# Moving the fourth GDN head behind all input projection tiles, and the late modulation vectors into the attention, in a two-layer hybrid transformer trunk

## The chip, the core and the metric

The kernel runs on one core of a Trainium2 chip. The metric is device time in microseconds (us) of one execution. The kernel before took 3876.38 us, the median of three runs that lay between 3871.95 and 3881.77 us.

In the text PE is TensorE (the matrix engine), PEld its weight loads, DVE is VectorE, ACT is ScalarE, POOL is GpSimd, and SP is the engine that issues nearly all DMAs (transfers to and from memory), in one queue and in order.

## The reference, cut to what matters

Each of two layers mixes tokens in three parallel ways from one input projection, and an MLP follows. There are 1024 latent tokens and 256 context tokens, 1024 features, all in fp32.

```python
for l in range(DEPTH):                      # DEPTH = 2
    sh1, sc1, gt1, sh2, sc2, gt2 = adaln(c, w_ada[l], b_ada[l])      # six modulation vectors
    h_lat = rms_norm(x, g_attn_pre[l]) * (1.0 + sc1) + sh1
    # hybrid_mixer: p = h @ w_in, split by columns into
    #   GDN  : 4 heads of 128, gated delta rule in chunks, forward and backward
    #   LRU  : a linear recurrence over 256 channels, forward and backward
    #   MLA  : 4 heads of attention over 1280 keys
    y_lat = concat([gdn_out, rl * gelu(..), a_l]) @ w_out
    x = x + gt1 * rms_norm(y_lat, g_attn_post[l])
    h = rms_norm(x, g_mlp_pre[l]) * (1.0 + sc2) + sh2
    x = x + gt2 * rms_norm(sq_relu_mlp(h, w_mlp1[l], w_mlp2[l]), g_mlp_post[l])
```

The first two of the six vectors (shift and scale, numbers 0 and 1) are needed before the input projection. Numbers 2 (gate), 3 and 4 (shift and scale of the MLP's norm) are first needed after the output projection of the same layer; number 5 later still. The context takes the same path, with vectors of its own, and its output is not needed in the second layer.

## The kernel before, in words

Activations lie transposed, features on the 128 partitions, tokens along the row, in three blocks: "c" (256 context tokens), 0 and 1 (512 latent tokens each). A large matmul is three fp32r products of high and low parts (`mm3`, line 230): eight contraction steps times three products, 24 matmuls for each block, 72 for a tile of 128 output features over all three blocks. A weight tile is loaded by SP (`wr`, two buffers), split by ACT into `wh` and by POOL into `wl` (line 138).

The order of instructions on each engine is fixed when the program is built. A scheduler places them by priority, and priority follows the order in which the Python code emits the operations. A stretch under `later()` gives its priority back, so the operations emitted in it are interleaved with those that follow.

Start. The three blocks are normalized, then `ada_pe` (line 260 on) computes modulation vectors 0 and 1: for each of eight contraction steps and each vector one `wa` load of 512 KB and two matmuls of 32x512 (line 273), at the end four transposes (line 283). A list `self.bg` holds such steps in waiting; `tick(n)` (line 322 on) adds n to a counter `self.due` and runs as many steps as it allows. At the start `tick(99)` runs the 17 steps of vectors 0 and 1. Then `run` puts the 26 steps of vectors 2, 3 and 4 into `bg`, to be run by later ticks: `weight` ticks with `self.rate` (0 in this stage), `mla_attend` ticks 1 for each of its key chunks (line 1022).

Mixer (lines 1033 to 1142). There are 24 input projection tiles: one with the GDN's gates, four per GDN head (`tiles(h)`: k, q, v and the output gate z), two pairs for the LRU (`xtile`), and three for the attention's latents (`kvq`: one for keys and values, two for queries). In layer 1 two gelu tiles and one z tile stand ahead of the rest. Tiles k, q, v go through a convolution on DVE (line 147), SiLU and transposes (line 441 and 460), and to memory.

`head(h)` is the gated delta rule of one head: decay matrices (lines 622 to 646), inversion of ten triangular 128x128 matrices per direction (`gdn_invert`; its core is a forward substitution of 60 dependent DVE operations on `X` and `T`, lines 138), ten steps of scan per direction (`gdn_scan`, lines 764 to 788, each a chain PE, DVE, PE, ACT, PE), and `gdn_y` with the transposes of line 819. It uses PSUM banks a, b and c.

`lru` has 20 segments of 256 tokens, each a chain of some 20 operations on ACT, DVE and POOL with a `lr<-lx` load in front and, in the first ten, an `lh<-lr` store behind (line 881). `mla_open` and `mla_prep(h)` prepare keys, queries, values and the row maxima of head h (26 DVE reductions per head in layer 0, 24 in layer 1, line 983), `mla_attend(h)` computes scores (lines 1012 to 1014), exponentials on ACT and the product with V (line 1027), 22 chunks per head in layer 0 and 20 in layer 1. After the GDN heads and the attention the output projection reads all eight groups of features.

Before the change the mixer emits: `tiles(0) head(0) tiles(1) head(1) tiles(2) head(2) xtile(0) xtile(1) tiles(3) head(3) kvq()`, then `mla_open`, `mla_prep(0)`, the LRU (under `later`), `mla_prep(1)`, `mla_attend(0)` and so on. So each head's chain runs beside the projection tiles emitted after it.

Of the kernel before, what the change touches and what calls it, by code (L numbers as in the profile page):

```python
# [43 lines left out]
class Trunk:  # L44
# [277 lines left out]
    def tick(self, n):  # L322

        self.due = self.due + n if self.bg else 0
        with self.later():
            while self.bg and self.due >= 1:
                self.due -= 1
                self.bg.pop(0)()


    def S(self, n):
# [701 lines left out]
    def mixer(self, L, hs, obl):  # L1033

        nc = self.nc
        l, last = L.l, L.l == DEPTH - 1
        pk = {}
        other = "left" if self.side == "right" else "right"
        sp = self.sp = self.pool("sp", other)
        yd = [self.dram(f"y{i}") for i in range(8)]  # L1040

        d = pk["krba"] = self.dram("krba")
        ba = sp.tile([P, NCH, 16], F32, name=self.nm("ba"))

        def evac(b, ps):
            c0, w = GRP[b]
            t = self.T()[:, :ps.shape[-1]]
            self.act(t, ps)
            self.keep(d, b, t)
            pt = self.G((P, 4, P))  # L1050
            for i in range(w):
                nc.tensor.transpose(pt[:, i, 0:32], t[0:32, i * P:(i + 1) * P], self.ident[0:32, 0:32])
            nc.vector.tensor_copy(ba[:, c0:c0 + w, :], pt[:, 0:w, 0:16])
        self.cur = ("s", (self.tp, 4), ["st"])
        zd = [self.dram(f"z{h}") for h in range(NH)]
        lg = [self.dram(f"lg{t}") for t in range(2)]

        if l:
            for t in range(2):
                self.gelu_tile(L, hs, 6 + t, obl, lg[t])  # L1060
            self.z_tile(L, hs, 8, obl, zd[0])
        self.w_in_tile(L, hs, 0, [0, 1, "c"] if l else BL, evac)
        self.gdn_coeffs(L, ba)
        gp = self.gp = self.pool("gp", other)
        self.XAT = gp.tile([P, NCH, 64], F32, name=self.nm("XAT"))
        nc.gpsimd.memset(self.XAT, 0.0)
        kd, xg = [], []

        def tiles(h):
            i0 = 12 + 3 * h  # L1070
            kd.append((self.qk_tile(L, hs, i0, 3 * h + 1, BL, f"k{h}", True),
                       self.qk_tile(L, hs, i0 + 1, 3 * h, obl, f"q{h}"),
                       self.v_tile(L, hs, i0 + 2, 3 * h + 2, BL, f"v{h}")))
            if h or not l:
                self.z_tile(L, hs, 8 + h, obl, zd[h])

        def head(h):
            with self.actor("g", (gp, 2), ["c"]):
                o = self.gdn_head(L, h, *kd[h], last)
                self.gdn_y(o, kd[h][1][1], zd[h], obl, yd[h])  # L1080

        def xtile(t):
            xg.append((self.lx_tile(L, hs, 4 + t, t, f"lx{t}"), lg[t]))
            if not l:
                self.gelu_tile(L, hs, 6 + t, obl, lg[t])

        def kvq():
            pk["kvn"] = self.kv_tile(L, hs, 1, "kvn")
            pk["cqn"] = self.cq_tiles(L, hs, 2, obl, "cqn")
        for h in range(3):  # L1090
            tiles(h)
            head(h)
        xtile(0)
        xtile(1)
        tiles(3)
        head(3)
        kvq()
        self.close(self.ap)
        side = self.side
        mp = self.mp = self.pool("mp", side)  # L1100
        self.lw = mp.tile([P, 2, 2, 2, P], F32, name=self.nm("lw"))
        nc.sync.dma_start(self.lw, self.I["lru_w"][l])
        mq = self.pool("mq", side)
        self.cur = ("s", (self.tp, 4), ["st", "b"])
        self.mla_open(L, pk, mq, not last)
        kqv = [self.mla_prep(L, 0, mq, not last)]
        self.cur, mine = self.main, self.cur
        with self.later():
            self.lru(L, [x for x, _ in xg], [g for _, g in xg], obl, yd[4:6])
        self.cur = mine  # L1110
        kqv.append(self.mla_prep(L, 1, mq, not last))
        self.mla_attend(0, kqv[0], not last, yd[6])
        kqv.append(self.mla_prep(L, 2, mq, not last))
        self.mla_attend(1, kqv[1], not last, yd[6])
        kqv.append(self.mla_prep(L, 3, mq, not last))
        self.close(mq)
        self.close(gp)
        self.close(sp)
        self.side = "left" if side == "right" else "right"
        self.ap = self.pool("ap", self.side)  # L1120
        ys = {b: [self.A(b) for _ in range(8)] for b in obl}

        def load(i):
            for b in obl:
                s, n = BLK[b]
                a = ys[b][i]
                nc.sync.dma_start(a[:, 1, :].bitcast(F32), yd[i][:, s:s + n])
                self.act(a[:, 0, :], a[:, 1, :].bitcast(F32))
                self.tt(a[:, 1, :], a[:, 1, :].bitcast(F32), a[:, 0, :].bitcast(F32), ALU.subtract, nc.gpsimd if i % 2 else None)
        for i in range(4):  # L1130
            load(i)
        self.mla_attend(2, kqv[2], not last, yd[7])
        load(4)
        load(5)
        load(6)
        self.mla_attend(3, kqv[3], not last, yd[7])
        load(7)
        self.cur = self.main
        self.close(mp)
        self.lp = self.xp = self.pool("lp", side)  # L1140
        return ys
# [290 lines left out]
```

## Time and profile before

| | us |
|---|---|
| median of three runs | 3876.38 |
| the profiled execution | 3882.76 |
| its span, first to last instruction | 3881.0 |
| PE busy | 3515.5 (91%) |
| DVE busy | 2099.4 (54%) |
| ACT busy | 1646.9 (42%) |
| POOL busy | 1315.2 (34%) |

Stages of the profiled execution, in us from the span's start, by the first and last matmul of each kind: modulation vectors on PE 26 to 123; layer 0 projection tiles 123.5 to 704; LRU, attention and the rest of head 3 until the output projection starts at 1041; MLP. Layer 1: projection tiles until 2668 (the transposes of its gate tile at 2191), LRU and attention until 3025.

How to read the profile: busy time is what an engine's instructions cover. Matmuls are pipelined, so busy PE is not PE at its peak. Releasers of a wait are inferred from semaphores. PEclk is the share of full TensorE clock that was granted. In a row of a timeline the first number is the start, the second the duration of the merged group, and in brackets stands the idle time ahead of it with what ended it. In a row of windows stand the stretch, its length, and per engine the busy time with the number of instructions, then the granted clock, the share of DMA busy and GB/s. In a row of groups stand, behind the bar, busy time, mean duration in ns, and idle time of the engine ahead of them.

### The profile page before, as it was taken

The numbers are of one execution on the slowest core, as the hardware profiler recorded it, in microseconds if no ns is written. First come the engines' busy times: TensorE is split into PE (matmuls) and PEld (weight loads), VectorE is DVE, ScalarE is ACT, GpSimd is POOL, SyncE is SP. The second block draws the span as 40 slices with busy tenths as digits, with TensorE's granted clock in tenths as the row PEclk, the third lists the DMA queues.
The fourth block names the chain that finished last, engine by engine and source line by source line (L and its number), as shares of the span: only waits on it lengthen the run. The fifth ranks groups of instructions, "written<-read, shape, count | busy, mean of one in ns | idle before, by whom it ended". The sixth has DMA issues, their size and how long they took to land. (4 is left out here: it accounts for less than half of the span.)

```text
span 3881.0 us, 51471 instructions
## 1 busy us (share of the span) xinstructions
PE 3515.5 (91%) x19236; PEld 2749.3 (71%) x19236; DVE 2099.4 (54%) x4351; ACT 1646.9 (42%) x3477; POOL 1315.2 (34%) x919
## 2 busy tenths in 40 slices
PE   4899989788998999999997989996798999999998
PEld 1577777455586888888877777774454778888886
DVE  5377677667437145555266586677676271422124
ACT  3355544555445331222354455444555463222242
POOL 3112212335476221111375421113335574222254
PEclk8899999899899999999998999997798999999999
DMA  6322212201433222322434322212002433311143
GB/s 236 120 84 82 85 59 77 81 22 49 126 114 109 66 82 87 93 90 85 130 114 130 97 85 85 80 63 97 29 18 79 145 102 96 100 47 46 49 137 102
DMA packets 164922, 347.13 MB, mean 89 GB/s; under 512 B 15552, under 2 KB 74304, under 8 KB 164672
## 3 DMA queue, kind: packets, MB, share of 16 engines
q1 hardware_dynamic: 164672, 343.85, 27.8%
q8 instruction: 151, 2.47, 0.3%
q14 instruction: 99, 0.81, 0.1%
HBM read 277.99 MB, written 65.80 MB: 89 GB/s over the span
## 5 line engine op out<-in xcount | busy, mean ns | idle before, releaser
L138 POOL TENSOR_TENSOR wl<-wr,wh 128x1024 fp32r<-128x1024 f32 x280 | 681.8, 2435 | 1703.7 <-ACT wh L135 953.1
L230 PE MATMUL mm<-A,wh 128*128 128x512 f32 (+1 forms) x3008 | 710.1, 380 | 2.9 <-POOL A L138 2.3
L135 ACT ACTIVATE wh<-wr 128x1024 fp32r<-128x1024 f32 x288 | 304.8, 1058 | 838.0 <-PE mm L230 325.8
L230 PEld LDWEIGHTS mm<-A,wh 128*128 128x128 f32 x3008 | 524.8, 195 | 97.1 <-POOL A L138 2.7
L138 DVE TENSOR_TENSOR hid<-T,hid 128x512 fp32r<-128x512 f32 (+1 forms) x160 | 171.6, 1075 | 451.6 <-ACT hid L135 451.6
L230 PE MATMUL mm<-A,wl 128*128 128x512 f32 (+1 forms) x1504 | 362.0, 374 | 1.4 <-DVE wl L138 1.4
L230 PE MATMUL mm<-hid,wh 128*128 128x512 f32 (+1 forms) x1280 | 302.7, 377 | 8.9 <-ACT T L135 6.8
L230 PEld LDWEIGHTS mm<-A,wl 128*128 128x128 f32 x1504 | 260.4, 191 | 48.4 <-DVE wl L138 1.6
L230 PEld LDWEIGHTS mm<-hid,wh 128*128 128x128 f32 x1280 | 227.7, 191 | 57.5 <-ACT T L135 7.2
L147 DVE SCALAR_TENSOR_TENSOR T<-raw,sm,T 128x512 f32<-128x512 f32 (+4 forms) x240 | 182.0, 759 | 49.3 <-ACT raw L135 25.5
L138 DVE TENSOR_TENSOR acc<-acc,mm 128x512 f32<-128x512 f32 (+1 forms) x140 | 88.5, 632 | 216.6 <-PE mm L230 215.9
L230 PE MATMUL pd<-A,wh 128*128 128x512 f32 (+1 forms) x704 | 193.7, 403 | 0.0
L230 PE MATMUL plr<-A,wh 128*128 128x512 f32 (+1 forms) x800 | 185.3, 383 | 0.0
L135 ACT ACTIVATE T<-T 128x512 f32<-128x512 f32 (+1 forms) x243 | 141.6, 583 | 98.2 <-DVE T L147 72.2
L1027 PE MATMUL pd<-Pt,V 128*128 128x512 f32 (+1 forms) x336 | 167.9, 620 | 8.8 <-ACT Pt L135 4.7
L138 POOL TENSOR_TENSOR S<-S,T 128x512 f32<-128x512 f32 (+1 forms) x126 | 162.8, 1294 | 38.0 <-ACT T L135 34.3
L230 PE MATMUL pb<-A,wh 128*128 128x512 f32 (+1 forms) x800 | 173.0, 367 | 1.2 <-ACT wh L135 1.2
L230 PE MATMUL mm<-hid,wl 128*128 128x512 f32 (+1 forms) x640 | 166.4, 378 | 8.1 <-DVE wl L138 8.1
L147 DVE SCALAR_TENSOR_TENSOR ada<-wa,sil,ada 128x256 f32<-128x256 f32 x392 | 166.3, 488 | 6.4 <-DMA wa<-in_w_ada_dram 6.4
L230 PEld LDWEIGHTS plr<-A,wh 128*128 128x128 f32 x800 | 143.6, 188 | 31.3
L230 PE MATMUL plr<-hid,wh 128*128 128x512 f32 (+1 forms) x640 | 153.2, 381 | 13.0 <-DVE hid L138 9.9
L147 DVE SCALAR_TENSOR_TENSOR lr<-lr,lr 128x256 f32<-128x256 f32 x218 | 108.3, 507 | 91.4 <-POOL lr L138 85.8
(365 smaller groups left out, 6848.1 us busy)
## 6 DMA issues: line engine op xcount, KB each, us to landing
wr<-in_w_mlp_dram SPq DMA_DIRECT2D x208, 512.0 KB, 3.6
wa<-in_w_ada_dram SPq DMA_DIRECT2D x96, 512.0 KB, 3.7
wr<-in_w_in_dram SPq DMA_DIRECT2D x48, 512.0 KB, 3.7
wr<-in_w_out_dram SPq DMA_DIRECT2D x32, 512.0 KB, 3.6
A<-y SPq DMA_DIRECT2D x32, 256.0 KB, 3.3
xm<-acc SPq DMA_DIRECT2D x32, 256.0 KB, 3.7
x<-xm SPq DMA_DIRECT2D x16, 512.0 KB, 6.4
kT<-k SPq DMA_DIRECT2D x8, 640.0 KB, 4.2
```

The source lines that it names most:

```text
L135: return self.nc.scalar.activation(out, in_, f, **kw)
L138: return (eng or self.nc.vector).tensor_tensor(out, a, b, op=op)
L147: return self.nc.vector.scalar_tensor_tensor(out, a, s, b, op0=op0, op1=op1)
L230: mm = nc.tensor.matmul(ps, w[wi][:, wk, :], a[:, ai, :], start=n == 0, stop=n == last)
L1027: nc.tensor.matmul(po, V[:, c, :], p, start=ci == 0, stop=ci == len(chunks) - 1)
```

## The change

Two edits. First, `tick` sets `due` to 0 when `bg` has run empty. Before, `tick(99)` left 82 of its 99, which the first tick of the mixer (with n = 0) spent on all 26 steps of vectors 2, 3 and 4 at once, ahead of the first projection tile. Now they wait in `bg` for the ticks of `mla_attend(0)`, and the last few for `mla_attend(1)`.

Second, the order of the mixer: `kvq` stands between `tiles(1)` and `head(1)`, `xtile(0)` ahead of `head(2)`, and `head(3)` behind everything that projects, in front of `mla_open`. The pool of the hidden states is closed, and the pools of LRU and attention opened, ahead of `head(3)`. Since head 3 uses the banks a, b and c, `mla_open` and the preparation of attention heads 0 and 1 take their PSUM tiles from banks st and d instead of st and b; from `mla_attend(0)` on it is st and b again.

```diff
             while self.bg and self.due >= 1:
                 self.due -= 1
                 self.bg.pop(0)()
+        if not self.bg:
+            self.due = 0
...
-        for h in range(3):
-            tiles(h)
-            head(h)
+
+        tiles(0)
+        head(0)
+        tiles(1)
+        kvq()
+        head(1)
+        tiles(2)
         xtile(0)
+        head(2)
         xtile(1)
         tiles(3)
-        head(3)
-        kvq()
         self.close(self.ap)
...
         mq = self.pool("mq", side)
-        self.cur = ("s", (self.tp, 4), ["st", "b"])
+        head(3)
+        self.cur = ("s", (self.tp, 4), ["st", "d"])
         self.mla_open(L, pk, mq, not last)
         kqv = [self.mla_prep(L, 0, mq, not last)]
...
         kqv.append(self.mla_prep(L, 1, mq, not last))
+        self.cur = ("s", (self.tp, 4), ["st", "b"])
         self.mla_attend(0, kqv[0], not last, yd[6])
```

On PE, at the end of vectors 0 and 1 (`pb`), the program before goes on with vectors 2 and 3 (`pc` from the loads `wa`):

```order
L273 MATMUL pb_325<-wa_386,sil 32x512 x2
L283 MATMUL pb_392<-cst,T_390 128x128 x4
L273 MATMUL pc_520<-wa_521,sil 32x512 x2
L273 MATMUL pc_520<-wa_525,sil 32x512 x2
L273 MATMUL pc_520<-wa_529,sil 32x512 x2
```

The changed program goes on with the first projection tile (`mm` from the activations `A` and the weight `wh`):

```order
L273 MATMUL pb_325<-wa_386,sil 32x512 x2
L283 MATMUL pb_392<-cst,T_390 128x128 x4
L230 MATMUL mm_526<-A_402,wh_522 128x256
L230 MATMUL mm_526<-A_406,wh_522 128x256
L230 MATMUL mm_526<-A_410,wh_522 128x256
```

48 matmuls of line 273 and 8 transposes have left this place.

On DVE, in the middle of head 3's forward substitution of layer 0 (`T<-X` and `X<-X,T` in turn), the program before mixes in the small operations of a norm (`n4s`) and a scaling (`T` with `sm`) of `kvq`:

```order
L138 TENSOR_TENSOR T_5825<-X_5776 128x234
L138 TENSOR_TENSOR n4s_6549<-n4s_6548,n4s_6550 128x4
L138 TENSOR_TENSOR X_5776<-X_5776,T_5825 128x18x13
L138 TENSOR_TENSOR n4s_6549<-n4s_6549,n4s_6548 128x4
L138 TENSOR_TENSOR T_5825<-X_5776 128x238
L147 SCALAR_TENSOR_TENSOR n4s_6548<-n4s_6549,n4s_6548 128x4
L138 TENSOR_TENSOR X_5776<-X_5776,T_5825 128x17x14
L138 TENSOR_TENSOR T_5825<-X_5776 128x240
```

The changed program mixes in the row maxima of attention head 0 (`mx`) and LRU operations (`lr`):

```order
L138 TENSOR_TENSOR T_6163<-X_6114 128x238
L147 SCALAR_TENSOR_TENSOR lr_6962<-lr_6969,lr_6962 128x256
L138 TENSOR_TENSOR X_6114<-X_6114,T_6163 128x17x14
L985 TENSOR_REDUCE mx_6854<-pd_6858 128x1
L138 TENSOR_TENSOR T_6163<-X_6114 128x240
L985 TENSOR_REDUCE mx_6854<-pst_6861 128x1
L138 TENSOR_TENSOR X_6114<-X_6114,T_6163 128x16x15
L985 TENSOR_REDUCE mx_6854<-pst_6867 128x1
```

In all, between the first and the last of the 60 operations, 26 maxima, 7 LRU operations of line 147, 2 of line 860 (862 in the changed kernel), one scan and some ten operations of rotary embedding and query splitting stand in the changed program. On PE head 3's first transposes stand directly behind the last projection matmul, and the whole preparation of attention heads 0 and 1 and the matmuls of six LRU segments stand within head 3; of the attention's own products only 20 matmuls stand ahead of its end.

On SP, during `mla_attend(0)` of layer 0, the program before has LRU loads and stores and the attention's output:

```order
L881 DMA lh_1187_7080<-lr_7229 128x256
L942 DMA wq_8476<-in_w_uq_dram 128x2x128
L842 DMA lr_7292<-lx_790_4680 128x256
L881 DMA lh_1188_7081<-lr_7264 128x256
L1031 DMA y_111_510<-T_8057 64x512
L842 DMA lr_7327<-lx_813_4892 128x256
```

The changed program has the loads `wa` of the modulation vectors between them:

```order
L883 DMA lh_1158_6961<-lr_7144 128x256
L271 DMA wa_7915<-in_w_ada_dram 128x1024
L271 DMA wa_7926<-in_w_ada_dram 128x1024
L271 DMA wa_7936<-in_w_ada_dram 128x1024
L271 DMA wa_7947<-in_w_ada_dram 128x1024
L1033 DMA y_111_510<-T_7978 64x512
L844 DMA lr_7207<-lx_856_5221 128x256
L271 DMA wa_7957<-in_w_ada_dram 128x1024
```

Such a load waits for the buffer `wr` that a matmul of an earlier step frees, and the stores and loads behind it in the queue wait with it.

## The prediction

> **What bounds the kernel now.** I read the page first, then the windows of each stage, then timelines at the stage borders, and groups of lines within the stages that the change touches. The page:
>
> ```profile
> span 3881.0 us, 51471 instructions
> PE 3515.5 (91%) x19236; PEld 2749.3 (71%) x19236; DVE 2099.4 (54%) x4351; ACT 1646.9 (42%) x3477; POOL 1315.2 (34%) x919
> PEclk8899999899899999999998999997798999999999
> ```
>
> PE is busy 91% of the span, so what can be won lies in the 365 us in which it is not. The granted clock has dips at the start and at two thirds of the span, where PE sits idle too. The windows cut by stage say where the idle time is (the numbers behind the length are busy us of PE, PEld, DVE, ACT, POOL, then clock, DMA share, GB/s). Layer 0: vectors 0 and 1; vectors 2 to 4; projection tiles; kvq with head 3, the end of these; then the first and the last part of LRU and attention, and these as a whole:
>
> ```profile
> 0.00:53.50 53.50, 23.11 (x97) 8.90 (x98) 32.05 (x115) 15.33 (x29) 13.20 (x16) 1.00 0.78 284
> 53.50:123.50 70.00, 41.86 (x107) 5.40 (x105) 24.96 (x44) 18.82 (x34) 16.76 (x14) 0.60 0.57 175
> 123.50:704.50 581.00, 532.14 (x4274) 444.02 (x4275) 388.65 (x1000) 289.26 (x837) 109.61 (x70) 0.97 0.25 82
> 620.00:704.50 84.50, 78.61 (x774) 65.75 (x773) 62.24 (x195) 34.63 (x94) 16.23 (x12) 0.98 0.19 59
> 704.50:780.00 75.50, 48.35 (x187) 30.59 (x187) 50.12 (x123) 41.47 (x111) 33.93 (x40) 0.73 0.21 69
> 860.00:1041.50 181.50, 153.12 (x485) 90.24 (x485) 122.98 (x210) 98.62 (x211) 84.84 (x107) 0.90 0.21 62
> 704.50:1041.50 337.00, 275.05 (x937) 166.68 (x937) 227.56 (x430) 184.33 (x418) 145.14 (x182) 0.87 0.18 54
> ```
>
> Layer 1: projection tiles from the gate tile on; LRU and attention; of these the stretch in which head 3 runs nearly alone; and the attention proper:
>
> ```profile
> 2191.00:2668.00 477.00, 436.09 (x3378) 356.43 (x3376) 334.62 (x859) 237.93 (x680) 79.84 (x45) 0.96 0.24 81
> 2668.00:3025.00 357.00, 275.69 (x1220) 171.93 (x1221) 241.26 (x476) 185.35 (x421) 141.68 (x171) 0.84 0.16 49
> 2668.00:2783.00 115.00, 60.44 (x515) 46.09 (x516) 81.06 (x199) 59.57 (x164) 45.43 (x57) 0.71 0.18 58
> 2806.50:3025.00 218.50, 199.78 (x676) 119.11 (x677) 144.63 (x246) 116.14 (x237) 87.63 (x103) 0.93 0.15 45
> ```
>
> Idle PE: 49 us in 581 of layer 0's projection, 41 in 477 of layer 1's; 62 in 337 and 81 in 357 of the two tails (so I call LRU and attention together). In layer 1, 55 of the 81 lie where head 3 has lost its cover. The 70 us for vectors 2 to 4 hold 42 us of PE at a clock of 0.60.
>
> **The start.** The end of the activations' last split, the pace of the vector steps, their end, the first projection matmuls, and the second tile:
>
> ```profile
> 73.07 4.77 DVE L138 TENSOR_TENSOR A<-xin,A 128x512 fp32r<-128x512 f32 x6
> 75.71 1.05 PE L273 MATMUL pc<-wa,sil 128*32 128x512 f32 x4 [1.64 <-DMA wa<-in_w_ada_dram]
> 84.37 1.92 PE L273 MATMUL pc<-wa,sil 128*32 128x512 f32 x4 [1.63 <-DMA wa<-in_w_ada_dram]
> 122.19 0.69 PE L283 MATMUL pc<-cst,T 64*128 64x64 f32 x4 [0.69 <-ACT T L135]
> 123.51 3.78 PE L230 MATMUL mm<-A,wh 128*128 128x256 f32 x16 [0.63 <-ACT wh L135]
> 140.96 0.88 PE L230 MATMUL mm<-A,wh 128*128 128x256 f32 x6
> ```
>
> ```profile
> 655.81 3.89 PE L230 MATMUL mm<-A,wh 128*128 128x512 f32 x16
> ```
>
> The activations are whole at 77.8, the projection starts at 123.5: PE waits for loads of vectors that nobody needs yet. In the changed program block c can start while blocks 0 and 1 are still split; what is left at 77.8 is at most the 8 products of block 1 with the last low parts and the 8 behind them, 16 times 0.243 us (3.89 by 16) or 4 us. So tile 1 begins near 83 in place of 141: a gain of 57. The next weight's split on POOL ends before that, as POOL's last split of `A` is over when DVE's is. If the split of the first weight gets in front of the activations' splits on POOL, it costs some us: bounds 48 to 62.
>
> **The vectors in the attention.** 24 steps and 8 transposes go where PE is the busier engine. A step is one row of x4 above: 1.05 us, or 1.92. The group says what PE paid in the old place:
>
> ```profile
> L273 PE MATMUL pc<-wa,sil 128*32 128x512 f32 x96 | 40.0, 969 | 26.1 <-DMA wa<-in_w_ada_dram 25.5 <-DVE ada L138 0.7
> ```
>
> 40 us busy, 25.5 idle for the loads. In the attention the clock was 0.90 to 0.93, so I take the fast step: 24 times 1.05 and 2 for the transposes, 27 us. Bounds: 5, if most of it fills PE's waits there, and 48, if all steps run slow. The Trainium skill, "TensorE: Matmul & The Clock Gate" (section What's actually happening), says that the clock is halved after an idle window of about 3.4 us. The two durations above, a factor of 1.8 apart, agree; by that rule alone, with a PE that goes idle around each load, the sum would have 48 in place of 27. That end is already among the bounds.
>
> The loads pass through SP's queue, and only two buffers hold them; the loads' own pace is a rival below. What waited for the vectors, the norm behind the output projection, is hundreds of us later: nothing.
>
> **Head 3 out of the projection.** Its matmuls move from the projection stage into the tail, which alone changes nothing in the sum. What changes is PE's idle time. In the projection stage 19 tiles now lie beside three heads instead of four, so each head has six or seven tiles (at 16 times 0.243 and 8 times half of it for each third of the products, about 15 us each) beside a chain of some 112 us (next part). These stages become matmul-bound. The idle time left comes from matmuls that wait for DVE's convolution, and that stays. I take 8 us less in layer 0, 4 in layer 1; bounds 25 less to 10 more in both together.
>
> **The tail.** Now head 3 starts only when the last projection matmul is issued, so its whole chain lies in the tail. Its length, from head 0, which ran beside projection tiles:
>
> ```profile
> 208.23 0.38 PE L622 MATMUL pa<-cst,gv 128*128 128x128 f32 x2
> 232.72 0.17 DVE L138 TENSOR_TENSOR T<-X 128x30 f32<-128x30 f32 x1
> 270.90 0.19 DVE L138 TENSOR_TENSOR X<-X,T 128x30 f32<-128x30 f32 x1
> 284.70 0.49 PE L768 MATMUL pa<-vt,N 128*128 128x128 f32 x2
> 320.18 0.49 PE L788 MATMUL pc<-X,at 128*128 128x128 f32 x2
> ```
>
> 24 us to the substitution, 38 in it, 14 to the scan, 36 in that: 112. In the tail DVE has other things mixed in:
>
> ```profile
> L138 DVE TENSOR_TENSOR T<-X 128x30 f32<-128x30 f32 (+14 forms) x240 | 96.8, 403 | 3.8
> L138 DVE TENSOR_TENSOR X<-X,T 128x30 f32<-128x30 f32 (+14 forms) x240 | 93.9, 391 | 3.8
> L983 DVE TENSOR_REDUCE mx<-pst 128x1 f32<-128x512 f32 (+1 forms) x52 | 30.2, 582 | 4.4 <-PE pst L982 4.0
> L147 DVE SCALAR_TENSOR_TENSOR lr<-lr,lr 128x256 f32<-128x256 f32 x110 | 54.2, 501 | 48.6 <-POOL lr L138 46.2 <-ACT lr L135 1.7
> ```
>
> The 60 operations of one head take 24 us (190.7 by 8). The order puts between them 26 maxima (15 us), ten LRU operations (5) and about ten for rotary embedding and query (estimated at 0.6 each, as the maxima, 6), so 50 us, and with waits for POOL (0.4 us per LRU operation, 48.6 by 110) 55. With LRU work in the inversion's second part (14 to 18) and maxima in the scan (36 to 43) the chain is 24 + 55 + 18 + 43 = 140 until the attention goes on. That is first late now where the projection's tiles were.
>
> What PE does in these 140 us: head 3's matmuls (about 45, an estimate: the 78.6 us busy from 620 to 704.5 less three tiles of 15 and some 7 for their norms leave 27, and half of a scan's 36 lay behind 704), two of four preparations and six of 20 LRU segments. By the groups of the tail:
>
> ```profile
> L982 PE MATMUL pst<-K,Q 96*128 96x512 f32 (+1 forms) x52 | 27.2, 524 | 13.4 <-DVE mx L983 8.6 <-DVE T L138 4.3 <-ACT Q L135 0.2
> L982 PE MATMUL pb<-K,Q 96*128 96x512 f32 (+1 forms) x52 | 27.2, 524 | 11.6 <-DVE T L138 6.5 <-DVE mx L983 3.1 <-ACT Q L135 1.8
> L956 PE MATMUL pst<-cqn,wq 128*128 128x256 f32 (+1 forms) x32 | 14.6, 588 | 10.5 <-ACT T L135 10.5
> L845 PE MATMUL plr<-lr,lw 128*128 128x256 f32 x80 | 24.8, 420 | 1.6 <-DMA lr<-lx 1.6
> ```
>
> These and smaller ones make about 95 us for all preparations: half is 47, six segments 7, so 100 us of work and 40 idle. Behind it comes the attention, whose waits were DVE's maxima (25 idle in the two rows of line 982); half of the maxima are then done. The windows give 28 us idle in 181.5 and 19 in 218.5; I take 25 and 20. So the idle time of the tail is 65 in place of 62 in layer 0 (+3). In layer 1 the chain starts alike, but less of the old one was hidden: 45 + 20 in place of 81; half of the maxima's relief was there already, so I count 10 less, not 16.
>
> **The sum.** Start -57, vectors +27, projection idle -8 and -4, tails +3 and -10: -49 us. Against the profiled execution, 3882.76, that gives 3834; it ran 6 us above the median, 3876.38, and against that it gives 3827. I take 3830. About 0.3% (12 us) is what a measurement of this kernel can tell from no change.
>
> **Rivals.** First, head 3's chain sets the tail longer than the projection gains (slower). Layer 1 of before shows a head 3 that had only LRU and preparation beside it:
>
> ```profile
> 2633.25 0.71 PE L634 MATMUL pc<-kT 128*128 128x128 f32 x4 [2.16 <-DMA kT<-k]
> 2806.81 0.63 PE L1012 MATMUL mm<-Q,K 97*128 97x512 f32 x1
> 648.12 2.43 POOL L138 TENSOR_TENSOR wl<-wr,wh 128x1024 fp32r<-128x1024 f32 x1 [7.17 <-ACT wh L135]
> 648.25 2.32 DVE L138 TENSOR_TENSOR n4s<-n4s,n4s 128x4 f32<-128x4 f32 x1
> ```
>
> 174 us from its first products to the attention's first scores. Now a second preparation is to be done in it as well. At 185 us in both layers in place of 140 and 145 the tails are 85 longer, and the kernel takes 3915. It decides from about 165 on, where the whole gain is gone. For it: the order lets only 20 products of the attention run ahead of head 3's end. Against: in layer 1 the maxima and the key products already ran late behind kvq's round trip through memory, which is now long over. Also for it: the last two rows, in which a DVE operation on four elements takes as long as POOL's operation beside it, and LRU keeps POOL busy. The Trainium skill, "SBUF — State Buffer" (Who interferes with whom), says that a DVE instruction with two inputs in SBUF and a GpSimd one that reads SBUF block each other fully; the trace agrees in this pair. Two LRU segments' worth of POOL operations, at half their 0.75 us each an estimate of 5 to 10 us per layer, would not decide it alone. Chance 0.17.
>
> Second, the vectors' loads hold up the attention. In the old place 24 steps took 69 us (53.5 to 122.9), 2.9 us a step, with the same two buffers; the order spreads them over about as much PE work, and the SP queue has LRU stores and loads between them, which wait for DVE. If PE waits one us a step and runs slow steps half of the time, this costs 35 us more: 3865, at the border of no change. Chance 0.15.
>
> Third, the new cover is better than I think: the tails' idle time falls to 45 in layer 0 and 35 in layer 1, and the projection loses 25: 3830 - 20 - 36 - 13 gives 3761. For it: the 55 us hole in layer 1. Against: DVE's chain. Chance 0.15.
>
> Fourth, the start isn't won, as the first tile waits for something else. The order has nothing in between, and the activations are there at 77.8. The kernel takes 3830 + 57, or 3887. Chance 0.03. That leaves 0.50 for the forecast, with 3805 to 3855 as its own range.
>
> **Chances and range.** Faster by over 0.3% (under 3865): the forecast, the third, and about a third of the second: 0.70. Within 0.3%: most of the rest of the second and the lower end of the first: 0.12. Slower: 0.18. The range reaches down over half of the third (3780) and up to the lower half of the first (3890).
>
> **What would show it.** Right: the first projection matmul near 60 and the second tile near 83; no `pc<-wa` before the attention; projection stages of 540 and 460 us; from the last projection matmul to the end of head 3's scan 140 us, with DVE over 80% busy in the substitution; tails of about 395 and 350 us. Wrong: a substitution of over 70 us, PEld waiting for `wa` by more than 15 us in all, or a projection stage with as much idle time as before would each move the sum by its size; a tile 1 that starts after 100 would refute the first term.

## The result and the profile after

The changed kernel takes 3837.9 us (median of four runs, 3833.4 to 3843.8), the kernel before 3877.8 us in the same comparison: a ratio of 0.9899 with a 95% interval of 0.9879 to 0.992, so 40 us less (31 to 47). Forecast were 3830 us with a range of 3780 to 3890. The profiled execution of the changed kernel has a span of 3831.6 us.

The page of the changed kernel:

```profile
span 3831.6 us, 51475 instructions
PE 3501.0 (91%) x19236; PEld 2746.6 (72%) x19236; DVE 2093.5 (55%) x4351; ACT 1645.2 (43%) x3477; POOL 1310.3 (34%) x919
PEclk9999998899999999999998999997998999999999
```

PE is busy 14.5 us less than before with the same 19236 matmuls, and waits 330.6 us in place of 365.5. The granted clock has lost its dip at the start, and the one at two thirds of the span is narrower.

The windows of the changed kernel by stage: from the end of vectors 0 and 1 to the second tile; projection from the second tile on; LRU and attention (the tail) of layer 0; output projection and MLP; projection of layer 1 from the gate tile on; its tail; the rest:

```profile
53.70:86.03 32.33, 22.88 (x78) 16.87 (x79) 26.10 (x38) 19.46 (x36) 23.94 (x16) 0.74 0.12 39
86.03:607.85 521.82, 483.45 (x3702) 402.92 (x3701) 340.72 (x884) 261.12 (x758) 96.15 (x62) 0.98 0.25 85
607.85:994.86 387.01, 322.54 (x1536) 189.85 (x1534) 272.05 (x551) 208.99 (x494) 150.24 (x187) 0.91 0.27 84
994.86:2145.60 1150.74, 1107.26 (x5674) 932.88 (x5672) 572.86 (x1018) 417.52 (x654) 463.55 (x257) 0.98 0.32 103
2145.60:2605.85 460.25, 420.45 (x3244) 347.68 (x3244) 316.60 (x809) 225.95 (x636) 73.48 (x41) 0.97 0.24 80
2605.85:2975.23 369.38, 292.34 (x1351) 180.75 (x1350) 257.11 (x525) 197.33 (x463) 143.53 (x175) 0.86 0.17 51
2975.23:3831.60 856.37, 828.61 (x3563) 666.52 (x3561) 276.08 (x411) 298.79 (x408) 346.23 (x166) 0.98 0.29 93
```

The kernel before, cut at the same events:

```profile
53.70:140.96 87.26, 59.10 (x184) 19.99 (x183) 25.38 (x46) 21.92 (x38) 21.50 (x16) 0.65 0.51 161
140.96:704.50 563.54, 514.70 (x4197) 429.36 (x4196) 388.23 (x998) 286.16 (x833) 104.86 (x68) 0.97 0.24 81
704.50:1041.30 336.80, 274.85 (x936) 166.48 (x936) 227.36 (x430) 184.33 (x418) 144.94 (x182) 0.87 0.18 54
1041.30:2191.80 1150.50, 1104.38 (x5675) 930.59 (x5673) 574.38 (x1018) 418.09 (x655) 463.06 (x257) 0.98 0.33 103
2191.80:2668.00 476.20, 435.29 (x3375) 356.04 (x3374) 334.62 (x859) 237.41 (x679) 79.84 (x45) 0.96 0.24 81
2668.00:3024.60 356.60, 275.29 (x1219) 171.57 (x1220) 241.26 (x476) 185.13 (x420) 141.68 (x171) 0.84 0.16 49
```

Row by row (the length, the second number): the second tile starts 54.9 us earlier; the rest of layer 0's projection is 41.7 shorter and its tail 50.2 longer; the MLP is the same; layer 1's projection is 16 shorter and its tail 12.8 longer. The waits of PE, length less busy, went from 48.8 to 38.4 and from 62.0 to 64.5 in layer 0, from 40.9 to 39.8 and from 81.3 to 77.0 in layer 1. Together 49 us between the two profiled executions; the medians lie 40 apart, as the one profiled execution lay 5 us above its kernel's median and the other 4 below.

Head 3 of layer 0 in the changed kernel, from the last projection matmul to the end of its scan on PE, and the first and the last operation of its substitution on DVE:

```profile
605.88 2.03 PE L230 MATMUL pd<-A,wl 128*128 128x512 f32 x8
746.45 0.49 PE L790 MATMUL pc<-X,at 128*128 128x128 f32 x2
```

```profile
633.30 0.20 DVE L138 TENSOR_TENSOR T<-X 128x30 f32<-128x30 f32 x1
686.88 0.19 DVE L138 TENSOR_TENSOR X<-X,T 128x30 f32<-128x30 f32 x1
```

139 us for the chain and 54 for the substitution; 140 and 55 were forecast. Of the other signs that the prediction names, the first projection product stands at 57.3 us (near 60 forecast) and the first of the vectors' products at 766, in the attention; the projection stages are 522 and 460 us long (540 and 460), the tails 387 and 369 (395 and 350).

### The profile page after: what moved, and what is told of

It is laid out like the page before. It is cut to its first block, busy times and chain, and to the rows that moved or that the text cites. A ratio compares the mean times of both kernels' runs of the same rounds, so it can differ in the third digit from the quotient of the medians.

```text
span 3831.6 us, 51475 instructions
## 1 busy us (share of the span) xinstructions
PE 3501.0 (91%) x19236; PEld 2746.6 (72%) x19236; DVE 2093.5 (55%) x4351; ACT 1645.2 (43%) x3477; POOL 1310.3 (34%) x919
## 5 line engine op out<-in xcount | busy, mean ns | idle before, releaser
L230 PE MATMUL mm<-A,wl 128*128 128x512 f32 (+1 forms) x1504 | 353.5, 371 | 1.2 <-DVE wl L138 1.1
L138 POOL TENSOR_TENSOR S<-S,T 128x512 f32<-128x512 f32 (+1 forms) x126 | 162.5, 1292 | 38.4 <-ACT T L135 35.3
L230 PE MATMUL plr<-hid,wh 128*128 128x512 f32 (+1 forms) x640 | 155.8, 386 | 10.1 <-DVE hid L138 10.0
```

What stands on the lines that cost most here:

```text
L138: return (eng or self.nc.vector).tensor_tensor(out, a, b, op=op)
L230: mm = nc.tensor.matmul(ps, w[wi][:, wk, :], a[:, ai, :], start=n == 0, stop=n == last)
```

## The experiments

The stages agree with the forecast in the main, but they don't say which edit brought what. All ratios are to the kernel before, run in between on the same chip; 0.001 is 3.9 us. Lengths of stages are read from one execution of each kernel, which lies up to 8 us off its median.

| kernel | median us | ratio | 95% interval |
|---|---|---|---|
| changed kernel (first comparison) | 3837.9 | 0.9899 | 0.9879 to 0.992 |
| changed kernel, again | 3835.9 | 0.9891 | 0.9874 to 0.9908 |
| only the vectors moved | 3838.0 | 0.9886 | 0.987 to 0.9902 |
| only the mixer's order | 3882.2 | 1.0001 | 0.9992 to 1.0011 |
| no vectors 2 to 4 | 3828.7 | 0.9864 | 0.985 to 0.9877 |
| kvq late | 3845.5 | 0.9914 | 0.9901 to 0.9928 |
| vectors in the preparation | 3843.2 | 0.9912 | 0.9894 to 0.993 |
| xtile(1) behind head 3 | 3841.6 | 0.9905 | 0.9886 to 0.9925 |
| products of the maxima three times | 3866.8 | 0.9971 | 0.996 to 0.9983 |
| LRU late | 3852.7 | 0.9938 | 0.9921 to 0.9954 |
| vectors in the projection | 3885.6 | 1.0024 | 1.0014 to 1.0035 |
| one load for all steps | 3859.5 | 0.9956 | 0.9939 to 0.9973 |
| old order, vectors in pairs | 3828.2 | 0.9882 | 0.9865 to 0.99 |

**The two edits apart.** The kernel before with the first edit alone:

```diff
                 self.bg.pop(0)()
+        if not self.bg:
+            self.due = 0
```

> The kernel before with the first edit alone: the counter is reset, so vectors 2 to 4 go to the attention, and the mixer keeps its old order. Theory (the terms add): the start is won as in the changed kernel, 55 us by its profile, and the 26 steps cost 27 us in the attention, so 28 us less than before, about 3850. Rival: in the old order PE waits more in the tail, and the steps fill these waits and cost 5 to 10; then 45 to 50 less, about 3830, and the second edit is worth nothing. Second rival: loads in SP's queue hold up the LRU and the attention, 40 or more for the steps; then 3862 or more.

And the changed kernel without it:

```diff
-        if not self.bg:
-            self.due = 0
```

> The changed kernel without the reset of the counter: vectors 2 to 4 stay ahead of the first projection tile, and only the order of the mixer is new. Theory: what is left of the gain when start and vectors are taken out, 49 less 28, about 21 us less than before by the pair of profiles (12 by the medians), so 3857 to 3866; nearly all of it in layer 0. Rival: the new order is worth nothing by itself (within 5 us of before), or costs, and the whole gain is the start's.

The first edit alone gives the whole gain, 44 us (38 to 50), the second alone nothing (3 less to 4 more): in both the rival's time came out. The start goes with the first edit: the second tile begins at 84.7 us with it alone and at 139.7 with the second alone, where it was 141.0. The rival's price for the vectors (5 to 10 us in the old order) isn't shown: the tail of layer 0 got 18.7 us longer there (windows below), in an execution 8 us above its kernel's median. The page and the windows of the second edit alone say where its gain went (projection from near the second tile on, tail of layer 0):

```profile
span 3880.5 us, 51489 instructions
PE 3527.2 (91%) x19236; PEld 2756.0 (71%) x19236; DVE 2104.7 (54%) x4351; ACT 1642.7 (42%) x3477; POOL 1310.1 (34%) x919
```

```profile
140.90:662.50 521.60, 483.29 (x3694) 402.93 (x3694) 342.29 (x884) 260.06 (x757) 95.09 (x62) 0.98 0.25 85
662.50:1041.90 379.40, 312.16 (x1432) 195.46 (x1430) 273.35 (x544) 206.15 (x491) 151.56 (x188) 0.86 0.17 52
```

The waits of PE did fall, from 365.5 us to 353.3 in the whole span, so by 12. But PE was busy 11.7 us longer with the same 19236 matmuls. Products that make the attention's keys (16 of one shape in the whole span), before and with the second edit alone, show where:

```profile
L948 PE MATMUL pst<-kvn,wk 128*64 128x512 f32 x16 | 8.6, 620 | 0.4 <-PE plr L845 0.4
L948 PE MATMUL pst<-kvn,wk 128*64 128x512 f32 x16 | 12.7, 891 | 0.0
```

891 ns for one in place of 620. In the whole span the 208 products for keys and values take 58.6 us of PE in place of 45.5, the 80 for queries 43.1 in place of 39.2: 17 us more, part of which other groups give back. The products of head 0's row maxima, before (757 to 788 us) and with the second edit alone (in the 52 us of the substitution, 694.5 to 746.5), take as long as they did, but wait more:

```profile
L982 PE MATMUL pb<-K,Q 96*128 96x512 f32 (+1 forms) x13 | 8.0, 616 | 4.9 <-DVE T L138 3.6 <-DVE mx L983 1.3
L982 PE MATMUL pst<-K,Q 96*128 96x512 f32 (+1 forms) x13 | 7.6, 582 | 4.8 <-DVE T L138 2.4 <-DVE mx L983 2.1 <-ACT Q L135 0.2
```

```profile
L982 PE MATMUL pd<-K,Q 96*128 96x512 f32 (+1 forms) x13 | 8.0, 614 | 8.3 <-DVE T L138 5.9 <-DVE mx L983 1.7 <-ACT Q L135 0.5
L982 PE MATMUL pst<-K,Q 96*128 96x512 f32 (+1 forms) x13 | 7.6, 582 | 9.7 <-DVE mx L983 5.2 <-DVE T L138 4.2 <-ACT Q L135 0.3
```

18.0 us of waits stand ahead of these 26 products in place of 9.7, and 28.5 ahead of all 104 of layer 0 in place of 25.0: the relief that the new order was to bring the maxima didn't come. The stretch of layer 0 in the changed kernel is granted 0.64:

```profile
639.85:691.85 52.00, 31.50 (x127) 19.93 (x126) 46.71 (x106) 13.86 (x30) 13.61 (x17) 0.64 0.03 8
```

DVE is busy 90% there and PE 61%. So preparation was moved into a stretch in which DVE sets the pace and PE runs slowly.

**What the vectors cost.** The changed kernel without their products:

```diff
-        self.bg = self.ada_pe(Ls[0], (2, 3), self.wp, "wr", 2, "c") + self.ada_pe(Ls[0], (4,), self.wp, "wr", 2, "c")
+        self.bg = []
+        nc.vector.memset(Ls[0].ada[:, 16:40, :], 0.0)
+        for v in (2, 3, 4):
+            self.ada_mods(Ls[0], v)
```

> The changed kernel without the products for vectors 2, 3 and 4 of layer 0 (left out, with their loads; zeros stand in their place). Theory: PE pays for each step what it is busy with, 26.4 us and 0.8 of waits by the profile, so 27 us less than the changed kernel, about 3811. Rival: the steps filled waits that come back, so only 5 to 15 less. Second rival: their loads held up LRU stores and attention in SP's queue, so 35 or more less.

0.9864 against 0.9891 and 0.9899: 10 to 14 us less, the first rival. The two profiled executions are equally long (3831.8 and 3831.6 us), so they can't place all of it. By stages (the changed kernel's tail of 387.0 against this one's below, and against 379.4 with the second edit alone) it is 5 to 8, though the group of the vector products is busy 27.0 us there:

```profile
L273 PE MATMUL pc<-wa,sil 128*32 128x512 f32 x96 | 27.0, 604 | 0.8 <-DMA wa<-in_w_ada_dram 0.8
```

The windows of the kernel without vectors: the whole tail, and in it the 82 us that would hold the vectors, and the last 82:

```profile
611.90:994.30 382.40, 316.38 (x1431) 197.71 (x1430) 272.76 (x544) 206.31 (x491) 151.37 (x188) 0.85 0.17 52
769.90:851.90 82.00, 73.30 (x238) 44.69 (x237) 55.93 (x96) 50.47 (x112) 38.89 (x51) 0.94 0.12 35
911.90:994.20 82.30, 73.67 (x227) 44.61 (x227) 47.41 (x71) 41.31 (x85) 28.82 (x35) 0.85 0.27 83
```

The same stretches of the changed kernel:

```profile
765.85:847.85 82.00, 76.87 (x262) 30.94 (x260) 46.52 (x83) 38.89 (x86) 33.16 (x45) 1.00 0.57 182
907.85:994.80 86.95, 77.02 (x263) 45.66 (x262) 57.91 (x92) 50.77 (x103) 38.15 (x45) 0.98 0.27 86
```

With the vectors the clock is 1.00 and 0.98 in place of 0.94 and 0.85, and PE is busy 322.5 us in place of 316.4: 27.0 for the vectors, and some 21 less for the rest. The second run of the changed kernel has the same clocks in these stretches. That the higher clock comes from the vectors was tried by the next kernel, which loads two tiles of their weights and not 24:

```diff
+            if ptag == "b" or not ws:
                 w = pool.tile([P, 1024], F32, tag=tag, bufs=bufs, name=self.nm("wa"))
...
+                ws[:] = [w]
+            w = ws[0]
```

> The changed kernel with one load of vector weights for vectors 2 and 3 and one for 4, used for all eight contraction steps in place of 24 loads (so these vectors have other values); the 48 products stay in the attention. Theory (what the vectors cost is PE's time, less what the higher clock gives back): the same as the changed kernel within 4 us, with the clock of the vectors' stretch near 1.0 again. Rival (the loads hold up LRU stores in SP's queue): as fast as the kernel without vectors, 8 to 13 us less than the changed one.

It is 22 to 25 us slower than the changed kernel, which neither theory had. With 22 loads fewer it shows no sign that the loads in SP's queue cost time, but its order of products differs too (below), so it doesn't isolate them. In its stretch PE no longer waits and the clock is 1.00, as the theory wants; but the clock behind doesn't stay up, and the products take longer:

```profile
765.60:847.60 82.00, 81.24 (x236) 27.93 (x234) 36.47 (x60) 33.01 (x72) 24.98 (x35) 1.00 0.11 33
907.60:1021.40 113.80, 98.70 (x307) 58.46 (x306) 74.05 (x116) 61.20 (x127) 46.82 (x58) 0.89 0.25 74
```

```profile
L276 PE MATMUL pc<-wa,sil 128*32 128x512 f32 x96 | 36.3, 602 | 0.0
```

Of the 26 us that PE is busy longer in its tail (348.6 against 322.5), 9 are the vectors' own. Its order differs: 28 of the 48 products stand apart from the other product of their step, 6 in the changed kernel, 32 in the kernel with the first edit alone. Rows of that last kernel show what that does: a product between others (two records), and a whole step (four records):

```profile
715.81 1.05 PE L273 MATMUL pc<-wa,sil 128*32 128x512 f32 x2
717.52 1.05 PE L273 MATMUL pc<-wa,sil 128*32 128x512 f32 x4 [0.66 <-DMA wa<-in_w_ada_dram]
```

1.05 us for one, and 1.05 for both together: the two products use different 32 columns of the array and run side by side if nothing stands between them. The Trainium skill, "TensorE: Matmul & The Clock Gate" (section The mechanism), says that each 32×32 tile of the array can hold weights of its own and compute a part of the output of its own, so that tiles overlap. The row of the whole step agrees; that a product in between undoes it is what the other row shows. The next experiment keeps the pairs together, in the old order with the first edit:

```diff
-                nc.tensor.matmul(ps[0][32 * q:32 * q + 32, :], self.sil[:, k, :],
+                with self.later(0 if ptag == "b" else -300):
+                    nc.tensor.matmul(ps[0][32 * q:32 * q + 32, :], self.sil[:, k, :],
...
```

> The kernel before with the counter's reset (as in the first experiment) and the two 32-column products of a vector step kept back to back by a priority raised by 300; the mixer keeps its old order. In the first experiment's order 32 of the 48 products stood apart from their partner, in the changed kernel 6. Theory of the pairs (two such products back to back take 1.05 us together, and 1.05 us each when another product stands between them; and this, not the mixer's order, made the vectors cheaper in the changed kernel): the 41 us of PE for the vectors fall to 26, and the kernel is 10 to 16 us faster than the first experiment, near 3825, so also faster than the changed kernel. Rival (the vectors are cheaper in the changed kernel since its tail has other waits and another clock): within 5 us of the first experiment, near 3838.

The vectors' group before the raised priority (first edit alone) and with it:

```profile
L273 PE MATMUL pc<-wa,sil 128*32 128x512 f32 x96 | 42.9, 643 | 5.2 <-DMA wa<-in_w_ada_dram 3.5 <-DVE T L138 1.7
```

```profile
L274 PE MATMUL pc<-wa,sil 128*32 128x512 f32 x96 | 28.7, 706 | 5.9 <-DMA wa<-in_w_ada_dram 3.6 <-DVE T L138 2.2
```

And the tail of layer 0, in the same order:

```profile
650.85:1006.40 355.55, 306.73 (x1041) 164.80 (x1041) 226.30 (x438) 186.74 (x420) 143.20 (x182) 0.92 0.28 86
```

```profile
643.80:994.20 350.40, 295.93 (x1042) 165.04 (x1042) 227.49 (x438) 185.93 (x420) 143.91 (x182) 0.89 0.28 87
```

The price of the pairs is confirmed, 14 us less of PE for the vectors. The kernel's time isn't, there the rival came out: the tail is 5 us shorter, as the waits grew from 48.8 to 54.5 and the clock fell from 0.92 to 0.89, and the ratios (0.9882 and 0.9886) can't be told apart. Nor can either from the changed kernel's, so no version tried that does all the work beats it beyond doubt.

Two other places for the vectors. Beside head 3's substitution, ticked by the row maxima of attention head 0, with the vectors' sums in bank mm:

```diff
+                    if not (L.l or h):
+                        self.tick(1)
                     pm = self.G()[:, :n2]
```

> The changed kernel with the 26 vector steps ticked by the row maxima of attention head 0 (one for each), so that they lie beside head 3's substitution, in bank mm. Theory of the clock (PE that waits there, 21 us of 52, is granted only 0.64 of full speed, and filler work gives part of its price back by a higher clock): the steps fill these waits, the stretch is granted 0.85 or more and the preparation in it runs faster, while the attention proper goes on like the kernel without vectors, with a clock of 0.85 to 0.94: 5 to 15 us less than the changed kernel. Rival (steps add their 27 us wherever they are, less what they fill): they delay the maxima on PE and DVE's chain with them, the tail of layer 0 gets 10 us longer.

0.9912, no faster and perhaps 5 to 8 us slower; layer 0's tail is 393.3 us, 6 longer, so nearer the rival. The 52 us of the substitution in this kernel:

```profile
646.80:698.80 52.00, 38.37 (x105) 11.62 (x104) 37.48 (x90) 7.33 (x16) 9.88 (x11) 0.70 0.48 154
```

PE waits 13.6 us there in place of 20.5, but DVE works only 37.5 of 52, and 13.4 us of its waits there are for the maxima's products: PE now holds up the maxima, and the whole substitution takes 65 us in place of 54. The clock is 0.70, far from the 0.85 of the theory. And in the projection:

```diff
-        self.bg = self.ada_pe(Ls[0], (2, 3), self.wp, "wr", 2, "c") + self.ada_pe(Ls[0], (4,), self.wp, "wr", 2, "c")
+        self.bg = self.ada_pe(Ls[0], (2, 3), self.wp, "wr", 2, "lr") + self.ada_pe(Ls[0], (4,), self.wp, "wr", 2, "lr")
+        self.rate = 1.5
```

> The changed kernel with vectors 2 to 4 ticked by the weights of layer 0's projection tiles (1.5 steps a tile, bank lr), where PE waits 38 us of 522 at a clock of 0.98. Theory: a step is 1.05 us of PE there and none of it brings back any clock, as the clock is high already; a third of the waits is filled. Against the kernel without vectors some 15 us, against the changed one, where vectors cost net 8 us, 7 us slower. Rival: the steps fill the waits for DVE's convolution wholly, and the kernel comes to within 4 us of the one without vectors, some 6 to 10 us faster than the changed one. Second rival: the loads take the weight buffers, tiles wait for weights, 15 us or more slower.

All the gain is gone, about 50 us more than the changed kernel; of what was expected the second rival (15 us or more) came out: PE waits 16.7 us in this projection for split weights, 10.1 of it ahead of the first tile. The first weight's tick puts steps ahead of the first tile, which starts at 76.0 and not 57.3, behind a wait for its own weight in the two buffers that the vectors now share; and the group takes its full price:

```profile
63.93 1.92 PE L273 MATMUL plr<-wa,sil 128*32 128x512 f32 x4 [3.58 <-DMA wa<-in_w_ada_dram]
75.97 3.78 PE L230 MATMUL mm<-A,wh 128*128 128x256 f32 x16 [10.12 <-ACT wh L135]
```

```profile
L273 PE MATMUL plr<-wa,sil 128*32 128x512 f32 x96 | 34.3, 637 | 9.2 <-DMA wa<-in_w_ada_dram 9.2
```

The start is 19 us later, and the products, of which the first three steps lie in it, are busy 34 us, as 20 of the 48 stand apart from their partner. On balance none of it is hidden: PE's waits from 112 us to the end of the projection (45.9 us of 557.2) are no fewer than the 38.4 in the whole projection of the changed kernel. Where PE is the bound, vectors cost what they are busy.

**The tail.** The three tiles of the latents back at the end of the projection:

```diff
         tiles(1)
-        kvq()
         head(1)
...
         tiles(3)
+        kvq()
         self.close(self.ap)
```

> The changed kernel with the three tiles of the attention's latents back at the end of the projection (behind the tiles of head 3, still ahead of head 3). Theory: head 3 keeps its place, but the first preparation has to wait for the norms of these tiles and their way through memory (in the layer 1 of before the first key product came 115 us after the last projection tile), so PE has nothing beside the substitution, and the kernel is 20 to 40 us slower than the changed one, about 3865. Rival: DVE, not the lack of products, sets the time of the tail, and the maxima that are not in the substitution make it shorter by what they took; then within 8 us of the changed kernel.

6 to 9 us slower than the changed kernel, at the edge of the rival and far from the theory, and the intervals overlap. Layer 0's tail is 13 longer (400.5), layer 1's not at all (367.9, against 369.4). The hole that I feared doesn't open: PE is busy 30.6 of the 52 us of the substitution, where it was 31.5. Real projection work beside head 3:

```diff
         head(2)
-        xtile(1)
         tiles(3)
+        head(3)
+        xtile(1)
         self.close(self.ap)
...
-        head(3)
```

> The changed kernel with the last LRU tiles (two in layer 0, one in layer 1) behind head 3 in the emission, so that real projection products lie beside its chain. Theory: these 30 and 15 us of work fill the 35 and 33 us in which PE waits from the last projection tile to head 3's scan and keep its clock up; the other heads lose nothing, as their stages are bound by products: 15 to 30 us less than the changed kernel. Rival: the preparation is put off by as much as the tiles take, so that the maxima come later and the attention waits for them; within 6 us of the changed kernel.

Within 6 us of the changed kernel: the rival. In layer 0 the tiles fill the first 32 us of the chain (PE busy 31.6, clock 1.00). The first and the last operation of head 3's substitution, and the 52 us from near its start:

```profile
619.29 0.17 DVE L138 TENSOR_TENSOR T<-X 128x30 f32<-128x30 f32 x1
661.77 0.55 DVE L138 TENSOR_TENSOR X<-X,T 128x30 f32<-128x30 f32 x1
```

```profile
620.90:672.90 52.00, 25.90 (x240) 12.72 (x239) 48.64 (x100) 23.79 (x49) 18.87 (x20) 0.61 0.30 89
```

The substitution takes 43 us in place of 54, as only 7 of the 26 maxima stand in it. The others come later, and the kernel as a whole gains nothing. In layer 1 the substitution stays at 54 us.

Filler in that stretch, the products of attention head 0's maxima computed three times:

```diff
-                    nc.tensor.matmul(pm, a[0:96, 0, i * P:(i + 1) * P], K[b2][0:96, 0, :], start=True, stop=True)
+                    for _ in range(3 if h == 0 else 1):
+                        nc.tensor.matmul(pm, a[0:96, 0, i * P:(i + 1) * P], K[b2][0:96, 0, :], start=True, stop=True)
```

> The changed kernel with each product for the row maxima of attention head 0 computed three times into the same bank in place of once, in both layers: 100 products more, at the 0.24 us of a fast 128x512 product and half of that for 256 columns some 20 us, at the slow clock 40. Nothing else changes. Theory of the clock: they fill PE's waits beside the substitution, the granted clock there goes from 0.64 to 0.85 or more, and the kernel is not slower than the changed one by over 5 us; it may be up to 10 faster. Rival (work on PE adds up, the clock follows something else): 20 to 40 us slower. Second rival: PE's waits there are filled, but DVE's chain waits for the repeated products, 10 to 20 us slower.

28 to 31 us slower than the changed kernel: the rival, work adds up (PE is busy 21.5 us longer in layer 0's tail). Some of the second rival is in it: head 3's substitution takes 59.6 us in place of 53.8, and DVE waits 7.1 us there for the maxima's products in place of 2.4. The window of the stretch:

```profile
643.00:695.00 52.00, 37.11 (x133) 28.07 (x131) 43.55 (x106) 12.50 (x28) 13.48 (x17) 0.67 0.03 10
```

The two longest waits in it, from the timeline:

```profile
651.03 0.98 PE L985 MATMUL pd<-K,Q 96*128 96x256 f32 x3 [6.58 <-DVE T L138]
655.75 0.98 PE L985 MATMUL pst<-K,Q 96*128 96x256 f32 x3 [3.74 <-DVE T L138]
```

The clock rose only to 0.67. The filler comes behind the long waits for DVE and not in them; that these hold the clock down was not shown. The Trainium skill, "TensorE: Matmul & The Clock Gate" (section What's actually happening), says that the clock is halved after an idle window of about 3.4 us, and these two waits are longer. But waits of that length are not needed here: in the kernel before, from 77.5 to 121.5 us, beside the vectors' loads, the clock was 0.54 and no wait of PE was longer than 1.9 us:

```profile
77.50:121.50 44.00, 28.87 (x64) 3.36 (x64) 0.95 (x7) 0.60 (x1) 0.00 (x0) 0.54 0.58 177
```

The last one puts the LRU behind the second preparation:

```diff
+        kqv.append(self.mla_prep(L, 1, mq, not last))
         self.cur, mine = self.main, self.cur
         with self.later():
             self.lru(L, [x for x, _ in xg], [g for _, g in xg], obl, yd[4:6])
         self.cur = mine
-        kqv.append(self.mla_prep(L, 1, mq, not last))
```

> The changed kernel with the LRU emitted behind the preparation of attention head 1, so that its operations leave head 3's substitution. Theory (DVE's queue sets the substitution: 60 operations of its own, 26 maxima, some ten LRU operations, DVE busy 46.7 us of 52): the substitution gets 5 us shorter per layer by the LRU operations that it no longer holds, and the tail by as much at most, since the LRU segments come back beside the attention; within 8 us of the changed kernel. Rival (POOL's operations beside DVE's make these slower): operations of the substitution get faster by 20% or more when POOL is idle beside them, 15 us or more per layer, and the kernel is 15 us faster.

It didn't test what it was made for: ten LRU operations still stand within each of the two substitutions, as the scheduler takes what is ready. It is about 15 to 18 us slower, which neither theory had. Layer 0's tail got 12 us longer; layer 1's got 13 shorter, and what follows it 11 longer, with waits of 4.0 and 4.6 us for the activations of the output projection, which come late:

```profile
2629.00:2985.50 356.50, 292.71 (x1348) 179.50 (x1347) 253.37 (x522) 192.64 (x457) 138.33 (x171) 0.86 0.16 49
2985.50:3853.30 867.80, 830.10 (x3565) 666.22 (x3563) 284.80 (x414) 301.93 (x414) 351.73 (x171) 0.98 0.30 93
```

A control stood beside the second group of runs:

> The changed kernel once more, to stand beside the next three on the same chip. By the profiles of the two kernels it is 49 us faster than before, by the medians 40; both theories expect 36 to 46 here.

41 us less by the medians, 42 by the ratio, as expected.

## Why the prediction held, and where it didn't

- **The start** (57 forecast; 141 less 83 is 58): 54.9 between the profiles. Right, and the only large gain. The first tile runs between the activations' splits from 57 us on, and nothing else stood in between.
- **The vectors in the attention** (27, bounds 5 to 48): mis-sized. PE is busy 27.0 us with them, as forecast, and waits 0.8 for their loads. But the tail is longer by only 5 to 8 us in the new order (the kernel by 10 to 14) and by 18.7 in the old one (355.5 against 336.8), where 32 products stood apart and the group was busy 42.9. The step that failed is taking PE's busy time as the price in a stretch in which the clock is not full: the other products took some 21 us less beside them. Of the clock, the two rows of vector steps read for it show the halving; the waits ahead of them were 1.6 us, shorter than the idle window that the prediction names beside them.
- **Projection waits** (-8 and -4): -10.5 and -1.1. **Tail waits** (+3 and -10): +2.5 and -4.3. The signs are right, and in the whole span the second edit takes 12 us of waits away where 19 were forecast.
- **The tail of the second edit** is where a step failed. The prediction took the preparation at the price of the old tail (about 95 us, half of it beside head 3's chain) and counted only waits; it says of head 3 that "Its matmuls move from the projection stage into the tail, which alone changes nothing in the sum". Head 3's matmuls aren't the ones that got slower (the 2296 products of all heads with tile `X` take 268.1 us in place of 273.6). The preparation is: its products for keys, values and queries took 17 us more, as those of the first two attention heads now lie beside head 3's chain, where PE is granted 0.82 and then 0.65 (32 and 52 us), and PE as a whole was busy 11.7 us longer with the same instructions. That ate the 12 us. So the edit that the forecast paid with 19 us is worth nothing, and the other one 44 in place of its 30. The two errors nearly cancel: that 3830 came out within 8 us of the measured 3838 is luck.
- **The rivals.** Head 3's chain is 139 and 141 us and not 185. PE waits 0.8 us for the loads `wa`; no run shows that they hold up anything else (with one load for all steps the kernel was slower, but in another order). The tails' waits didn't fall to 45 and 35 (64.5 and 77.0). The start was won.

**What stays open:** what sets the clock behind the vectors' stretch. It is 0.98 in both profiles of the changed kernel, 0.85 without vectors, 0.89 with the same products fed from one load, and 0.90 and 0.88 with kvq late and with the LRU late, where the same products stand at the same place. Vectors alone don't decide it, and no run here shows what does.

## What to carry to other kernels

Take the two halves of a change apart before believing a sum that came out right: here one half had all the gain. A stretch that is short of work on the matrix engine because another engine sets its pace can be a poor place for more matmuls: beside the substitution they ran at a low clock (0.61 to 0.70) and kept DVE waiting, while the attention took the vectors for a part of their time. Look for work that nobody needs yet ahead of a bound stage, and move that. The price of moved work is its time in the new place, and what it does to the neighbours' clock belongs to it.

## What the runs showed of the hardware that was not expected

Two products with 32 stationary columns each take 1.05 us together when they stand back to back, and 1.05 us each when another product stands between them (the groups of 96 records: 28.7 us with all pairs kept, 42.9 with 32 of 48 products apart). Filling PE's short waits brought little clock (0.64 to 0.67 with 18% more PE work in the stretch; waits of 6.6 and 3.7 us remained). The clock was also low, 0.54 over 44 us, where no wait was longer than 1.9 us. 27 us of added matmuls lengthened a stage by 5 to 8 us, with a clock of 0.91 in place of 0.85 over it.
